# The last quarter-products, the final norm and the stores in a fixed order, with the norm's factors in the last scaling

## The chip, the cores and the metric

The kernel runs on one core of a Trainium2 chip. The metric is the device time of one execution in microseconds (us), the median of several runs. In this text TensorE (PE in the profile) does the matmuls, VectorE (DVE) the elementwise arithmetic, ScalarE (ACT) activations and casts, GpSimd (POOL) some additions, and SyncE (SP) issues the loads and stores.

## What is computed

The reference is one step of a one-layer streaming encoder with 1,024 prompt tokens and 64 sample tokens, 1,088 in all, and a model width of 1,024. Only its end matters here: the SwiGLU block, whose down product is added to the residual stream, and the final RMSNorm with the factors `g_final`.

```python
def rms_norm(x, g=None):
    xf = x.astype(jnp.float32)
    y = xf * lax.rsqrt(jnp.mean(xf * xf, axis=-1, keepdims=True) + EPS)
    if g is not None:
        y = y * g.astype(jnp.float32)
    return y.astype(x.dtype)
...
def swiglu(x, g_ffn, w_gate, w_up, w_down):
    hn = rms_norm(x, g_ffn)
    return (jax.nn.silu(hn @ w_gate) * (hn @ w_up)) @ w_down
...
        hp = hp + swiglu(hp, g_ffn[l], w_gate[l], w_up[l], w_down[l])
...
    y_prompt = rms_norm(hp, g_final)
    y_sample = rms_norm(hs, g_final)
```

## The kernel before

Activations lie transposed: features on the 128 partitions, tokens along the free axis, so the stream is eight tiles `y[0]` to `y[7]` of 128 x 1,088, one for each block of 128 features. Prompt and sample tokens are worked on together. The tokens are cut into two halves of 544 columns (`HALF`), and a half into two quarters of 272 (`HC`). A product in full precision takes three passes: each operand is split into a high and a low part (`split`, L122: a cast on ScalarE, then a subtraction on VectorE, L124), and `mm3` (L147) runs high x high, high x low, low x high.

The instructions are written in Python in some order and a planner then places them: on each engine it takes what is ready in its own simulated timeline, in order of priority, which is the order of writing unless a block raises it (`high_priority`). Where a block stands under `issue_after(ins)`, its instructions on the engine of `ins` may not be placed ahead of `ins`. `in_order` (L855) does so with the last matmul of TensorE that was recorded in `last_mm`. On the chip each engine works through its queue in the order so found, and waits at the head of the queue for what an instruction needs.

The down product (`down`, L1426) runs over the 22 blocks of the hidden width in three groups. Most of it is done by a Strassen scheme of seven half-size products for a pair of feature blocks (`strassen`, L247). In the last group the scheme leaves out the products P2 and P4. With them left out, the second token half (columns 544 to 1,087) is complete after the scheme, and of the first half two partial products are missing; these are computed directly, in the two quarters, from weights that are loaded again (L1490 to L1497). This is the rest: for each quarter eight products of nine matmuls, one for each feature block (L1498 to L1507). A product's result lies in one of four bank pairs of PSUM (the pool `ps`, tag `q`), which is free again when VectorE has added the result to `y` (L1506).

When a feature block of a half or quarter is complete, `complete` (L1442) takes its square on ScalarE (L1446, L1449), adds it to a running sum on VectorE in `self.rstd` (L1450), and multiplies `y` by the factor g of each feature on ScalarE (L1451).

`final_norm` (L1515) then finishes a half or a quarter: matmuls of the sums with ones give each token's sum on the partitions (`token_rstd`, L306), six small steps give the inverse root, with one Newton step (L289 to L294: VectorE, the root on ScalarE, then four on VectorE), matmuls with the identity spread it over the partitions again (L1527), and ScalarE copies it to `self.rstd` (L1528). The whole stands under `high_priority`. `final_scale` (L1530) multiplies the eight tiles by it on VectorE (L1533) and stores each (L1534, issued by SyncE at L120). The order of writing is: rest products of the first quarter; norm and scaling of the second half; norm of the first quarter; rest products of the second quarter; its norm; scaling of the first quarter, then of the second. An activation at L1488 loads the table of the square root early.

## Time and profile before

| what | us |
| --- | --- |
| timed runs | 2256.48, 2258.14, 2258.49 |
| their median | 2258.14 |
| profiled execution | 2251.97 |
| its span from the first to the last instruction or transfer | 2250.1 |

The profiled execution is one run of its own; 1.87 us of it lie outside the span that the profile covers. All times of instructions below are microseconds from the start of this span. A row of a timeline has start, duration, engine, line of the kernel, operation, what it writes and reads with the shapes, how many instructions are merged in it, and in brackets the idle time of the engine ahead of it with what ended that time. A row of a table of groups has, behind the bar, busy time in all and mean nanoseconds of one, and then the idle time ahead. "Clock" is the share of its full clock that TensorE was granted.

### The profile page before, as it was taken

To read this page: it belongs to the slowest core of one execution; us is meant where nothing else is said; L and a number is where in the kernel's file an instruction comes from. 1 tells how busy PE (TensorE), PEld (TensorE's weight loads), DVE (VectorE), ACT (ScalarE), POOL (GpSimd) and SP (SyncE) were. 2 spreads that over 40 slices of the span, in tenths; PEclk is the share of its full clock that TensorE was granted. 3 is DMA by queue.
4 is the path that set the end of the run, shared out by engine and by line. 5 is a ranking of instruction groups with operands and counts; after the bars stand their busy time and mean duration, and the time that the engine had idled before them with its cause. 6 is when DMAs were issued, how large, how long until landed. Compare 5 with 4: busy or idle time off the path is not lost.

```text
span 2250.1 us, 41674 instructions
## 1 busy us (share of the span) xinstructions
PE 2172.4 (97%) x16382; PEld 2108.2 (94%) x16382; DVE 1594.2 (71%) x2656; ACT 896.2 (40%) x1921; POOL 689.0 (31%) x466
## 2 busy tenths in 40 slices
PE   7899999999999989999999999999999999999996
PEld 6899999999999977779999998999999999999996
DVE  8985878677687568875455565776777767777596
ACT  7333333435444355553233343333222223344344
POOL 1441534342253112220000000014555556434471
PEclk9999999999999989999999999999999999999997
DMA  5433344443445475326343111412342332475223
GB/s 199 159 120 109 111 129 130 132 130 113 169 139 187 143 242 164 111 67 222 121 153 113 39 66 59 143 62 91 122 148 79 101 131 85 152 258 192 86 84 108
DMA packets 182598, 290.84 MB, mean 129 GB/s; under 512 B 40290, under 2 KB 110850, under 8 KB 182402
## 3 DMA queue, kind: packets, MB, share of 16 engines
q1 hardware_dynamic: 177794, 279.26, 38.2%
q10 hardware_dynamic: 4608, 8.91, 1.1%
q8 instruction: 129, 2.11, 0.4%
q14 instruction: 67, 0.55, 0.1%
HBM read 196.95 MB, written 91.16 MB: 128 GB/s over the span
## 4 chain that ended last, share of the span: by engine, by line
PE 80%; DVE 10%; DMA 4%; issue 3%; ACT 2%; POOL 1%; SPq 0%; DVEq 0%; ACTq 0%; POOLq 0%
PE pq L205 15%; PE pq L208 15%; PE pq L206 15%; PE pd L149 8%; PE pd L150 8%; PE pd L151 8%; DVE wq L124 2%; PE pout L992 1%; PE pp L976 1%; DMA hl<-d_op 1%; PE pss L934 1%; DVE T L124 1%; DVE B L124 1%; PE pk L691 1%; DVE xg L1280 1%
## 5 line engine op out<-in xcount | busy, mean ns | idle before, releaser
L123 ACT CAST wq<-raw 128x512 fp32r<-128x512 f32 (+1 forms) x505 | 307.9, 614 | 572.1 <-PE pq L208 308.2
L124 DVE TENSOR_TENSOR wq<-raw,wq 128x512 fp32r<-128x512 f32 (+1 forms) x505 | 447.6, 890 | 107.7 <-ACT wq L123 105.7
L205 PE MATMUL pq<-T,wq 128*128 128x272 f32 x1832 | 501.3, 291 | 6.4 <-DVE u L252 3.1
L206 PE MATMUL pq<-T,wq 128*128 128x272 f32 x1832 | 497.7, 288 | 0.0
L205 PE MATMUL pq<-B,wq 128*128 128x272 f32 x1592 | 436.7, 292 | 11.7 <-ACT wq L123 10.5
L206 PE MATMUL pq<-B,wq 128*128 128x272 f32 x1592 | 435.1, 290 | 9.1 <-DVE B L124 8.9
L208 PE MATMUL pq<-T,wq 128*128 128x272 f32 x1832 | 382.6, 289 | 1.0 <-DVE wq L124 0.9
L183 POOL TENSOR_TENSOR raw<-raw 128x512 f32<-128x512 f32 (+1 forms) x59 | 81.6, 1383 | 899.7 <-DVE wq L124 615.2
L205 PEld LDWEIGHTS pq<-T,wq 128*128 128x128 f32 x1832 | 345.2, 188 | 7.2 <-DVE u L252 3.2
L206 PEld LDWEIGHTS pq<-T,wq 128*128 128x128 f32 x1832 | 348.5, 190 | 0.3 <-issue 0.3
L208 PE MATMUL pq<-B,wq 128*128 128x272 f32 x1592 | 333.5, 289 | 0.0
L206 PEld LDWEIGHTS pq<-B,wq 128*128 128x128 f32 x1592 | 304.4, 191 | 11.7 <-DVE B L124 11.3
L205 PEld LDWEIGHTS pq<-B,wq 128*128 128x128 f32 x1592 | 301.3, 190 | 12.4 <-ACT wq L123 10.5
L208 PEld LDWEIGHTS pq<-T,wq 128*128 128x128 f32 x1832 | 285.3, 188 | 2.4 <-DVE wq L124 1.7
L208 PEld LDWEIGHTS pq<-B,wq 128*128 128x128 f32 x1592 | 249.1, 189 | 0.5 <-issue 0.3
L252 DVE TENSOR_TENSOR u<-pq,u 128x544 f32<-128x544 f32 x177 | 127.7, 721 | 128.2 <-PE pq L208 127.5
L186 POOL TENSOR_TENSOR raw<-raw 128x512 f32<-128x512 f32 (+1 forms) x59 | 83.5, 1415 | 141.0 <-DVE wq L124 133.4
L563 DVE TENSOR_TENSOR stage<-pq,u 128x544 f32<-128x544 f32 x112 | 80.4, 718 | 29.1 <-PE pq L208 26.5
L962 POOL TENSOR_TENSOR t<-t,den 128x768 f32<-128x768 f32 (+2 forms) x34 | 47.9, 1409 | 167.5 <-DVE nm L950 58.7
L184 POOL TENSOR_TENSOR raw<-raw 128x512 f32<-128x512 f32 (+1 forms) x59 | 88.3, 1497 | 3.7
L1438 POOL TENSOR_TENSOR y<-u,y 128x544 f32<-128x544 f32 x38 | 63.0, 1664 | 73.6 <-DVE y L1436 51.8
L189 POOL TENSOR_TENSOR raw<-raw 128x512 f32<-128x512 f32 (+1 forms) x59 | 84.1, 1426 | 4.4
(356 smaller groups left out, 4669.8 us busy)
## 6 DMA issues: line engine op xcount, KB each, us to landing
hl<-d_op SPq DMA_DIRECT2D x85, 272.0 KB, 4.1
d_qkv<-stage SPq DMA_DIRECT2D x44, 272.0 KB, 2.1
d_op<-stage SPq DMA_DIRECT2D x44, 272.0 KB, 2.1
d_op<-ht SPq DMA_DIRECT2D x44, 272.0 KB, 3.3
raw<-w_gate SPq DMA_DIRECT2D x22, 512.0 KB, 3.4
raw<-w_up SPq DMA_DIRECT2D x22, 512.0 KB, 3.5
d_gate<-stage ACTq DMA_DIRECT2D x32, 272.0 KB, 2.3
raw<-w_down SPq DMA_DIRECT2D x16, 512.0 KB, 4.3
```

Source lines behind the costliest of these rows:

```text
L123: self.last_cast = self.nc.scalar.copy(hi, src).ins
L124: self.nc.vector.tensor_tensor(out=lo, in0=src, in1=hi.bitcast(F32), op=ALU.subtract)
L149: mm(ps, wh, xh, start=start, stop=False)
L150: mm(ps, wh, xl, start=False, stop=False)
L151: self.last_mm = mm(ps, wl, xh, start=False, stop=stop).ins
L184: tt(out=a21, in0=a21, in1=a22, op=add)
L186: tt(out=a11, in0=a22, in1=a11, op=sub)
L189: tt(out=a12, in0=a12, in1=a11, op=sub)
L205: mm(ps[:, c, :HC], w[:, 0, ks], x[:, 0, cs], start=start, stop=False)
L206: mm(ps[:, c, :HC], w[:, 0, ks], x[:, 1, cs], start=False, stop=False)
L208: self.last_mm = mm(ps[:, c, :HC], w[:, 1, ks], x[:, 0, c * HC:(c + 1) * HC], start=False, stop=stop).ins
L252: add = lambda out, a, b: nc.vector.tensor_tensor(out=out, in0=a, in1=b, op=ALU.add)
```

## The change

The block that finishes the kernel is written anew. `split` now gives back its VectorE instruction, and the last one is recorded in `last_queued`; `queued` writes an instruction of VectorE under `issue_after` of the one recorded before, so that these instructions keep the order of writing. TensorE's part stands under `in_order`. In `finish` the sixteen rest products run one after the other, j = 0 to 15. The half's sums and roots come behind product 5, its spread behind product 7, its eight scalings and stores one by one behind the products 8 to 15; the first quarter's sums and roots behind product 11, its spread behind product 14. The addition of a square comes one product later than the square. Behind the last product stand three scalings of the first quarter, the second quarter's norm, the other five, and the second quarter's eight.

The second quarter's norm (`wide_roots`) takes another way: two matmuls with the 128 x 128 ones, of the running sum and of the last square, give each token's sum on all partitions at once, and the root steps are then done on 128 x 272 instead of 128 x 3, with no spread and no copy.

The multiplication by g on ScalarE (L1451) is gone; `scale` does it together with the norm in one `scalar_tensor_tensor`. The number of stores and their sizes stay.

```diff
     def split(self, src, hi, lo):
         self.last_cast = self.nc.scalar.copy(hi, src).ins
-        self.nc.vector.tensor_tensor(out=lo, in0=src, in1=hi.bitcast(F32), op=ALU.subtract)
+        return self.nc.vector.tensor_tensor(out=lo, in0=src, in1=hi.bitcast(F32), op=ALU.subtract).ins
...
-            nc.scalar.mul(o, o, self.gains[:, 3, m:m + 1])
...
-            self.split(raw[:, :2 * n], q[:, 0, :2 * n], q[:, 1, :2 * n])
+            self.last_queued = self.split(raw[:, :2 * n], q[:, 0, :2 * n], q[:, 1, :2 * n])
             rest += [(m + i, q[:, :, i * n:(i + 1) * n], self.ops[("B21", "T4")[i]]) for i in range(2)]
-        for c0 in (0, HC):
...
-        for c0 in (0, HC):
-            self.final_scale(y, c0, HC)
+        self.finish(y, rest)
+
+    def queued(self, emit):
+        with self.tc.issue_after(self.last_queued):
+            self.last_queued = emit().ins
+
+    def finish(self, y, rest):
         nc = self.nc
+        tt, stt, ts = nc.vector.tensor_tensor, nc.vector.scalar_tensor_tensor, nc.vector.tensor_scalar
+        cols = [slice(0, HC), slice(HC, HALF), slice(HALF, T)]
+        squares, factors = {}, {}
+        bank = lambda: self.bank_pair()[:, 0, :]
+
+        def product(c, m, q, xs):
+            ps = bank()[:, :HC]
+            for k, x in enumerate(xs):
+                ks = slice(k * P, (k + 1) * P)
+                x = x.rearrange("p a (b c) -> p a b c", b=2)[:, :, c]
+                self.mm3(ps, q[:, 0, ks], q[:, 1, ks], x[:, 0], x[:, 1], k == 0, k == len(xs) - 1)
+            return ps
+
+        def grow(c, m, ps):
+            v = y[m][:, cols[c]]
+            self.queued(lambda: tt(out=v, in0=ps, in1=v, op=ALU.add))
+            sq = self.rstd[:, cols[c]]
+            if m:
+                sq = self.hl.tile([P, HALF], F32, tag="hl", name="sq")[:, :HC]
+            nc.scalar.activation(sq, v, AF.Square)
+            squares[c, m] = sq
+
+        def gather(c, m):
+            acc = self.rstd[:, cols[c]]
+            self.queued(lambda: tt(out=acc, in0=acc, in1=squares[c, m], op=ALU.add))
+
+        def sums(c):
+            spans = self.spans(cols[c].stop - cols[c].start)
+            ps = bank()[:, :2 * len(spans)].rearrange("p (t two) -> p t two", two=2)
+            for i, (a, w) in enumerate(spans):
+                a += cols[c].start
+                self.last_mm = nc.tensor.matmul(ps[:, i, :], self.rstd[:, a:a + w], self.ones[:, :2], start=True, stop=True).ins
             r = self.np.tile([P, 5], F32, tag="rf", bufs=2, name="rs_f")[:, :len(spans)]
+            factors[c] = r, spans, ps[:, :, 0]
+
+        def roots(c):
+            r, spans, ps = factors[c]
...
+            self.steps(r, v, t, ps)
+
+        def wide_roots(c, m):
+            ps = bank()[:, :HC]
+            mm = nc.tensor.matmul
+            mm(ps, self.ones, self.rstd[:, cols[c]], start=True, stop=False)
+            self.last_mm = mm(ps, self.ones, squares[c, m], start=False, stop=True).ins
+            v, t = (self.hl.tile([P, HALF], F32, tag="hl", name="wide")[:, :HC] for _ in range(2))
+            self.steps(self.rstd[:, cols[c]], v, t, ps)
+
+        def spread(c):
+            r, spans, _ = factors[c]
+            for part in ((0, 2), (2, 5)) if len(spans) > 4 else ((0, len(spans)),):
+                pb = bank()
+                a0, a1 = spans[part[0]][0], spans[part[1] - 1][0] + P
+                for i in range(*part):
                     at = spans[i][0] - a0
+                    self.last_mm = nc.tensor.matmul(pb[:, at:at + P], r[:, i:i + 1].broadcast_to([P, P]), self.ident,
+                                                    start=True, stop=True).ins
+                c0 = cols[c].start
+                nc.scalar.copy(self.rstd[:, c0 + a0:c0 + a1], pb[:, :a1 - a0])
+
+        def scale(c, k):
+            o = y[k][:, cols[c]]
+            self.queued(lambda: stt(o, o, self.gains[:, 3, k:k + 1], self.rstd[:, cols[c]], ALU.mult, ALU.mult))
+            self.store(self.io["o_y"][k, :, cols[c]], o)
+
+        for j in range(2 * KT):
+            c, m = divmod(j, KT)
+            ps = self.in_order(lambda: product(c, *rest[m]))
+            grow(c, rest[m][0], ps)
+            if (j - 1) % KT and j:
+                gather((j - 1) // KT, rest[(j - 1) % KT][0])
+            if j == 5:
+                self.in_order(lambda: sums(2))
+                roots(2)
+            if j == KT - 1:
+                self.in_order(lambda: spread(2))
+            if j == KT + 3:
+                self.in_order(lambda: sums(0))
+                roots(0)
+            if j == KT + 6:
+                self.in_order(lambda: spread(0))
+            if j >= KT:
+                scale(2, j - KT)
+        for k in range(3):
+            scale(0, k)
+        self.in_order(lambda: wide_roots(1, rest[-1][0]))
+        for k in range(3, KT):
+            scale(0, k)
         for k in range(KT):
+            scale(1, k)
+
+    def steps(self, out, v, t, ps):
+        nc = self.nc
+        stt, q = nc.vector.scalar_tensor_tensor, self.queued
+        q(lambda: nc.vector.tensor_scalar(v, ps, 1.0 / D, EPS, ALU.mult, ALU.add))
+        nc.scalar.activation(out, v, AF.Sqrt)
+        q(lambda: nc.vector.reciprocal(out, out))
+        q(lambda: nc.vector.tensor_tensor(out=t, in0=out, in1=out, op=ALU.mult))
+        q(lambda: stt(t, t, -0.5, v, ALU.mult, ALU.mult))
+        q(lambda: stt(out, t, 1.5, out, ALU.add, ALU.mult))
```

30 lines of the change are left out of this document (2 added, 28 removed).

## The prediction

> **What bounds the kernel now.** I read the page first, then a table by stages of the last 48 us, then those stages instruction by instruction on TensorE, VectorE and the store queue.
>
> ```profile
> span 2250.1 us, 41674 instructions
> PE 2172.4 (97%) x16382; PEld 2108.2 (94%) x16382; DVE 1594.2 (71%) x2656; ACT 896.2 (40%) x1921; POOL 689.0 (31%) x466
> ```
>
> TensorE is busy for 97% of the span, so the kernel as a whole is bound by its matmuls, and the change leaves those as they are. What it can win lies where TensorE isn't busy at the end:
>
> ```profile
> core 0: us, PE busy (x) PEld busy (x) DVE busy (x) ACT busy (x) POOL busy (x), PEclk, DMA share, GB/s
> 2202.40:2209.50 7.10, 4.23 (x29) 3.50 (x28) 5.99 (x8) 3.15 (x4) 2.85 (x2) 0.93 0.31 105
> 2209.50:2215.10 5.60, 5.59 (x24) 5.59 (x25) 4.18 (x9) 5.26 (x13) 1.82 (x2) 0.50 0.00 0
> 2217.90:2226.40 8.50, 4.50 (x33) 4.14 (x33) 6.00 (x19) 2.57 (x8) 0.00 (x0) 0.75 0.23 87
> 2226.40:2229.00 2.60, 2.60 (x13) 2.60 (x13) 2.60 (x6) 0.39 (x1) 0.00 (x0) 0.51 1.03 391
> 2229.00:2236.80 7.80, 7.79 (x63) 7.57 (x61) 6.73 (x18) 5.24 (x14) 0.00 (x0) 1.00 0.61 205
> 2236.80:2243.20 6.40, 2.71 (x12) 2.33 (x12) 2.06 (x8) 1.92 (x5) 0.00 (x0) 0.69 0.01 1
> 2243.20:2250.10 6.90, 0.00 (x0) 0.00 (x0) 2.91 (x8) 0.00 (x0) 0.00 (x0) 0.50 0.47 163
> ```
>
> Each row is a stretch, its length, busy time of each engine and the granted clock. The rest products of the first quarter run to 2217.9. Then 8.5 us pass in which TensorE runs only norm matmuls and waits, 10.4 us with the products of the second quarter, 6.4 us for its norm and 6.9 us for the last scalings and stores. At full clock 63 matmuls take 7.8 us, 0.124 us each, so a product of nine takes 1.12 us.
>
> ```profile
> 2207.35 0.36 PE L149 MATMUL pq<-B,wb 128*128 128x272 f32 x1 [2.02 <-DVE y L1436]
> 2209.51 0.59 PE L149 MATMUL pq<-T,wb 128*128 128x272 f32 x1 [0.69 <-DVE y L1436]
> 2217.84 1.17 PE L306 MATMUL pt<-ones,rstd 128*128 128x2 f32 x10
> 2220.33 0.93 PE L1527 MATMUL pb<-ident,rs_f 128*128 128x128 f32 x6 [1.32 <-DVE rs_f L294]
> 2225.19 1.62 PE L1527 MATMUL pb<-ident,rs_f 128*128 128x128 f32 x6 [2.68 <-DVE rs_f L294]
> 2226.46 0.57 PE L149 MATMUL pq<-B,wb 128*128 128x272 f32 x1
> 2236.51 0.29 PE L151 MATMUL pq<-T,wb 128*128 128x272 f32 x1
> 2238.75 1.06 PE L306 MATMUL pt<-ones,rstd 128*128 128x2 f32 x6 [1.96 <-DVE rstd L1450]
> ```
>
> The second quarter's first product starts at 2226.46, behind spreads that waited for VectorE (2.68 us for a small `rs_f`). VectorE and the store queue in the same stretch and at the end:
>
> ```profile
> 2222.97 0.72 DVE L1533 TENSOR_TENSOR rstd_f<-rstd_f,rstd 128x544 f32<-128x544 f32 x1
> 2224.89 0.15 DVE L294 SCALAR_TENSOR_TENSOR rs_f<-rs_t,rs_f 128x3 f32<-128x3 f32 x1
> 2224.96 3.26 DVE L1533 TENSOR_TENSOR y<-y,rstd 128x544 f32<-128x544 f32 x5
> 2228.49 2.55 DVE L1533 TENSOR_TENSOR y<-y,rstd 128x272 f32<-128x272 f32 x7
> 2243.20 0.44 DVE L1533 TENSOR_TENSOR rstd_f<-rstd_f,rstd 128x272 f32<-128x272 f32 x1 [2.16 <-ACT rstd L1528]
> 2243.56 2.55 DVE L1533 TENSOR_TENSOR y<-y,rstd 128x272 f32<-128x272 f32 x7
> 2243.67 0.33 SPq L120 DMA_DIRECT2D o_y<-rstd_f  x1
> 2244.12 3.55 SPq L120 DMA_DIRECT2D o_y<-y  x7
> ```
>
> That `rs_f` step stood behind scalings of the last half, at 2224.89. But the wait isn't empty time: the eight wide scalings and the first quarter's eight are done in its shadow, so only eight scalings are left for the end. There the queue sets the pace, not VectorE: seven scalings take 2.55 us (0.35 apart), seven stores 3.55 us (0.51 apart). The last issue ends at 2247.67, and 2.43 us later the span ends.
>
> **The change part by part.** *TensorE.* Everything up to 2217.84 is the same work. Into it go the norm matmuls of the half: the sums, ten instructions (1.0 us, as they stand at 2217.84), and the spread, ten instructions at the 0.13 us of the row at 2220.33, 1.3 us. The ninth product therefore starts at 2217.84 + 1.0 + 1.3 = 2220.1 instead of 2226.46. Eight products at full clock, 9.0 us, with six sums (0.6) and six spreads (0.8) between them, end at 2230.5, against 2236.8: 6.3 us earlier.
>
> *VectorE* doesn't keep up. What it does per instruction:
>
> ```profile
> L1450 DVE TENSOR_TENSOR rstd<-rstd,sq 128x272 f32<-128x272 f32 x14 | 6.1, 437 | 1.4 <-ACT sq L1449 1.3
> 1437.97 0.61 DVE L1244 SCALAR_TENSOR_TENSOR xg<-hx,gains,rstd 128x384 f32<-128x384 f32 x1
> 1438.50 0.55 DVE L278 TENSOR_TENSOR rstd_f<-rstd_f,sq 128x384 f32<-128x384 f32 x1
> 2219.05 0.17 DVE L289 TENSOR_SCALAR rs_v<-pt 128x5 f32<-128x5 f32 x1
> 2220.11 0.17 DVE L294 SCALAR_TENSOR_TENSOR rs_f<-rs_t,rs_f 128x5 f32<-128x5 f32 x1
> ```
>
> A narrow `tensor_tensor` takes 0.44 us, and the next one starts after 0.35 to 0.36 (the seven in 2.55 us above). The new scaling multiplies by a column of `gains` too; line 1244 has this form at 384 elements, 0.06 us longer than the `tensor_tensor` behind it. So I take 0.42 for a narrow scaling and, from the 0.64 pitch of the wide ones (five in 3.26 us), 0.70 for a wide one. The five small root steps take 1.2 us from 2219.05 to 2220.11 and its end. From the ninth product on VectorE has 8 adds (2.8), 7 additions of squares (2.5), 8 wide scalings (5.6) and one set of roots (1.3, with its waits): 12.2 us. The first add can start when the ninth product is done, 2220.1 + 1.1 + 0.2 = 2221.4, and the last wide scaling ends at 2233.6, 3.1 us behind TensorE. So VectorE is the bound here, and half of what TensorE wins is gone. The last product's own add, addition and wide scaling need 1.6 us of this, so a delay of TensorE behind the ninth product costs nothing up to 1.5 us and counts in full beyond; one ahead of the ninth product counts in full, since VectorE's row starts with it.
>
> *The last norm* swaps a chain for wider steps. Now: product end 2236.8, add, square, addition, sums at 2238.75, roots, spread, copy, first scaling at 2243.20, 6.4 us. After: the last square and two full-width sums on TensorE run while VectorE does the last wide scaling and three narrow ones, and the roots are taken on all 272 columns.
>
> ```profile
> 1274.31 1.08 PE L1202 MATMUL csss<-ck,qsm 128*64 128x256 f32 x4
> L1449 ACT ACTIVATE sq<-y 128x272 f32<-128x272 f32 x14 | 5.7, 423 | 1.5 <-DVE y L1506 1.3
> L1451 ACT ACTIVATE y<-y,gains 128x272 f32<-128x272 f32 x14 | 6.9, 512 | 0.1
> L291 DVE RECIPROCAL rr<-rr 128x2 f32<-128x2 f32 x16 | 2.6, 162 | 4.3 <-ACT rr L290 4.3
> L291 DVE RECIPROCAL rtok<-rtok 128x8 f32<-128x8 f32 x1 | 0.2, 185 | 0.0
> ```
>
> Two f32 matmuls are four instructions, 1.1 us at this width (1.08 for four of 256); with the square (0.42) and two handovers 1.6 us, hidden behind 0.7 + 3 x 0.42 = 2.0 us of scalings. Then, from 2233.6: three scalings to 2234.9, the affine step to 2235.3, the root on ScalarE (0.42 and two handovers of 0.04) to 2235.8. Nothing else of VectorE may go here, since its order is fixed. A reciprocal of 272 elements is not in the trace. If it runs like a `tensor_tensor`, 0.44 us; by the slope between 2 and 8 elements, 23 ns over six, 0.16 + 270 x 3.8 ns = 1.2, and with 10 ns of doubt on that slope 0.7 to 1.65. I take 1.0, inside the slope's band, and keep 0.44 and 1.65 as ends. Three dependent steps of 0.48 follow: 2238.3. The first scaling behind them ends at 2238.8.
>
> The Trainium skill speaks against the wide reciprocal: "VectorE: DVE Perf Modes", section "Walkthrough: the 8-slice pipeline in each mode", says that it runs as an iterative divide with a repeat count of 8. At its 0.96 GHz that is an estimate of 272 x 8 / 0.96 = 2.3 us, and the sum below would end 1.3 us later. The two rows here agree with something between: 23 ns where the rule gives 50.
>
> *Stores.* Behind that step 13 narrow scalings are left, where there are 8 now. VectorE needs 0.42 for each, the queue 0.51 for each issue, so the queue sets the end: 13 x 0.51 = 6.6, to 2245.5, and 2.4 us until the span ends: 2247.9. The eight wide stores go out earlier, one for every 1.4 us of VectorE, and hide.
>
> *ScalarE* loses 24 multiplications by the gains (0.51 us for a narrow one); it is busy 5.2 of 7.8 us in the last product stage, so that is worth nothing by itself.
>
> *Sum.* TensorE 6.3 us earlier, less 3.1 for VectorE's lag; then 2233.6 to the first free scaling and 13 stores: 2247.9 against 2250.1, 2.2 us less. The profiled execution took 2251.97, 1.87 around its span; the median of the timed runs is 2258.14, 6.2 us above it. I carry the difference over: 2258.14 - 2.2 = 2255.9.
>
> **The rivals.** *The early stalls go too (faster).* TensorE waits 2.02 and 0.69 us at 2207.35 and 2209.51 for additions that stand in VectorE's queue around the splits of the last weights:
>
> ```profile
> 2207.17 1.65 DVE L124 TENSOR_TENSOR wb<-raw,wb 128x768 fp32r<-128x768 f32 x1
> 2208.74 0.71 DVE L1436 TENSOR_TENSOR y<-pq,y 128x544 f32<-128x544 f32 x1
> ```
>
> Behind these waits 25 matmuls run at clock 0.50, 0.227 us each instead of 0.124, 2.5 us. These rows lie ahead of the fixed order. Without ScalarE's multiplications the planner may place splits and additions otherwise. All of it is worth 5.2 us: 2255.9 - 5.2 = 2250.7. Against it: the splits and the additions are written as before, and the weight loads that they wait for too.
>
> *The wide reciprocal is slow.* The rows bound it at 1.65, and if each element takes several times an addition's time the end slips by about 1 us: 2257. The Trainium skill's rule on the divide, named above, points this way.
>
> *The clock stays low (slower).* TensorE has clock 0.75 in the norm stage and 0.51 in the 2.6 us behind it. The new order puts 2.3 us of sums and spreads in one piece ahead of the ninth product. If the second eight products then ran at half clock, 72 x 0.103 = 7.4 us more and 1.4 for their norm matmuls, TensorE would end at 2239.3, and VectorE 1.6 us later instead of at 2233.6: 7.3 us, less the 2.2 won, 2263.2. With 1.5 us of cover and 2.2 won it is slower than before from 3.7 us of such delay on, some 36 matmuls at half clock. Against it: in the trace the half clock stands behind waits, and after 5.6 us of unbroken products it is full again; the spreads follow products at full clock. The Trainium skill ("TensorE: Matmul & The Clock Gate", section "Part 1: The HAM clock gate (the "warmup" mystery)") asks for about 3.4 us of idleness before it halves the clock; here 2.02 and 0.69 us of waits were enough.
>
> *The stall only moves.* The half's spread needs `rs_f` from VectorE, with two products (2.2 us) between its sums and the spread, and two additions, two squares' additions and the 1.2 us of roots in VectorE's queue meanwhile, 2.6 us. If it comes late TensorE waits again, up to the 2.68 us of now, and VectorE's wide scalings with it; the end then slips by 1 to 3 us: 2257 to 2259.
>
> **How the numbers follow.** Forecast 0.46, early stalls 0.18, slow reciprocal 0.18, low clock 0.10, moved stall 0.08. The forecast's own spread is 2 us either way (the reciprocal's ends, 0.6 us; the handovers on a queue of some 45 instructions; the pitch of 13 stores). With the early stalls below and half of the low clock left out, the range is 2250.0 to 2260.5. What a measurement of this kernel can tell from no change is about 0.2%, 4.5 us. Faster by more: nearly all of the early stalls (0.17) and a fifth of the forecast's spread (0.10), 0.27. Slower by more: 0.07 of the low clock and 0.02 of the moved stall, 0.09. Within: 0.64.
>
> **What would show it.** In the changed profile the ninth rest product should start near 2220 with no gap above 0.5 us, and clock 1.00 should hold to the sixteenth. VectorE should have no idle time above 0.5 us from there to the wide root steps, and TensorE should end its products some 3 us ahead of the last wide scaling. The wide reciprocal should show 0.44 to 1.65 us. The last 13 stores should stand 0.5 us apart. I am wrong if TensorE still waits between the two quarters, if additions still stand in front of TensorE and VectorE idles, or if the stretch ahead of 2209.5 has changed.

## The result, and the profile after

The changed kernel took 2250.41 us, the median of six runs (2246.01 to 2252.76), against 2259.95 for the kernel before in runs beside it: a ratio of 0.9952, interval 0.9935 to 0.9969. That is 9.5 us less, where 2.2 were predicted, and beyond both the forecast's own spread and the 0.2% that I called no change. Applied to the 2258.14 us that the prediction started from, the ratio gives 2247.3, below the lower end of its range, 2250.0. The profiled execution took 2246.01.

First the page of the changed kernel, its first lines, and the table by stages of its end (the columns are those shown for before).

```profile
span 2244.2 us, 41644 instructions
PE 2161.9 (96%) x16374; PEld 2097.0 (93%) x16374; DVE 1602.8 (71%) x2655; ACT 883.9 (39%) x1896; POOL 689.8 (31%) x466
```

```profile
core 0: us, PE busy (x) PEld busy (x) DVE busy (x) ACT busy (x) POOL busy (x), PEclk, DMA share, GB/s
2199.70:2205.20 5.50, 2.75 (x18) 2.35 (x19) 4.25 (x6) 2.49 (x4) 0.67 (x1) 1.00 0.50 143
2205.20:2209.00 3.80, 3.65 (x16) 3.35 (x17) 2.86 (x5) 1.20 (x3) 3.80 (x3) 0.56 0.00 0
2209.00:2216.00 7.00, 7.00 (x61) 7.00 (x60) 6.46 (x19) 3.68 (x10) 0.20 (x1) 1.00 0.01 2
2216.00:2226.60 10.60, 10.59 (x87) 10.37 (x85) 8.84 (x24) 3.67 (x10) 0.00 (x0) 1.00 0.31 123
2226.60:2234.70 8.10, 1.47 (x4) 0.68 (x4) 7.50 (x16) 1.29 (x3) 0.00 (x0) 0.68 0.46 167
2234.70:2244.20 9.50, 0.00 (x0) 0.00 (x0) 5.43 (x14) 0.00 (x0) 0.00 (x0) 0.50 0.56 192
```

The 8.5 us in which TensorE ran norm matmuls and waited are gone: from 2209.0 to 2226.6 it is busy throughout at clock 1.00. The work behind its last product, 8.1 us to the first free scaling and 9.5 to the end, is VectorE's and the stores'. Now the timeline of the changed kernel on TensorE, then on VectorE and on the store queue:

```profile
2205.22 0.36 PE L149 MATMUL pq<-B,wb 128*128 128x272 f32 x1 [2.06 <-DVE y L1436]
2211.59 1.17 PE L1540 MATMUL pq<-ones,rstd 128*128 128x2 f32 x10
2214.95 1.27 PE L1566 MATMUL pq<-ident,rs_f 128*128 128x128 f32 x10
2215.99 0.37 PE L149 MATMUL pq<-B,wb 128*128 128x272 f32 x1
2226.30 0.29 PE L151 MATMUL pq<-T,wb 128*128 128x272 f32 x1
2228.77 0.72 PE L1554 MATMUL pq<-rstd,ones 128*128 128x272 f32 x2 [2.18 <-DVE rstd L1532]
```

```profile
2228.63 0.78 DVE L1573 SCALAR_TENSOR_TENSOR y<-y,gains,rstd 128x544 f32<-128x544 f32 x1
2229.32 0.50 DVE L1573 SCALAR_TENSOR_TENSOR rstd_f<-rstd_f,gains,rstd 128x272 f32<-128x272 f32 x1
2230.56 0.44 DVE L1605 TENSOR_SCALAR wide<-pq 128x272 f32<-128x272 f32 x1
2231.49 1.85 DVE L1607 RECIPROCAL rstd<-rstd 128x272 f32<-128x272 f32 x1 [0.49 <-ACT rstd L1606]
2234.69 2.14 DVE L1573 SCALAR_TENSOR_TENSOR y<-y,gains,rstd 128x272 f32<-128x272 f32 x5
2237.17 2.97 DVE L1573 SCALAR_TENSOR_TENSOR y<-y,gains,rstd 128x272 f32<-128x272 f32 x7
2237.59 0.41 SPq L120 DMA_DIRECT2D o_y<-rstd_f  x1
2238.12 3.58 SPq L120 DMA_DIRECT2D o_y<-y  x7
```

The last wide scaling ends at 2229.41, 2.8 us behind TensorE's last product; the wide reciprocal takes 1.85 us; the last stores stand 0.51 us apart (3.58 for seven). The rest begins with a matmul that started at 2202.47 before and starts at 2199.73 now. From there to the end of the span it is 47.7 us before and 44.5 now: 3.2 us are won in this tail, and the other 2.7 us of the two profiles ahead of it.

Up to 2167 us every engine has the same instructions in the same order as before. From there on ScalarE lacks the multiplications and VectorE makes some additions of squares elsewhere, while TensorE's order is the same until the sixth rest product ends. These are the same two matmuls ahead of any difference, before and after:

```profile
2165.34 0.52 PE L208 MATMUL pq<-T,wq 128*128 128x272 f32 x2 [0.19 <-DVE wq L124]
2161.83 0.52 PE L208 MATMUL pq<-T,wq 128*128 128x272 f32 x2 [0.20 <-DVE wq L124]
```

In this pair of profiles 3.5 us were won by the same instructions in the same order, and had to come from something else. The two programs differ in one more thing. The part of `roots` that the diff above leaves out reads

```python
            v = self.np.tile([P, 5], F32, tag="vf", bufs=2, name="rf_v")[:, :len(spans)]
            t = self.np.tile([P, 5], F32, tag="tf", bufs=2, name="rf_t")[:, :len(spans)]
```

Two new tags with two buffers each are four tiles of 20 bytes, given 32 bytes each, in the pool `norm`. That pool is opened near the front of the kernel, so all tiles that are laid out behind it on that side (the loaded weights `raw`, their split parts `wq`, sums, stages) lie 128 bytes further along each partition; the large operands `B` and `T` are laid out from the other side and stay.

### The profile page after: what moved, and what is told of

The parts are those of the page before. It is cut to its first block, busy times and chain, and to the rows that moved or that the text cites. A ratio compares the mean times of both kernels' runs of the same rounds, so it can differ in the third digit from the quotient of the medians.

```text
span 2244.2 us, 41644 instructions
## 1 busy us (share of the span) xinstructions
PE 2161.9 (96%) x16374; PEld 2097.0 (93%) x16374; DVE 1602.8 (71%) x2655; ACT 883.9 (39%) x1896; POOL 689.8 (31%) x466
## 4 chain that ended last, share of the span: by engine, by line
PE 80%; DVE 10%; DMA 4%; issue 2%; ACT 2%; POOL 1%; SPq 0%; DVEq 0%; ACTq 0%; POOLq 0%
PE pq L208 15%; PE pq L205 15%; PE pq L206 15%; PE pd L149 8%; PE pd L151 8%; PE pd L150 8%; DVE wq L124 2%; PE pout L992 1%; DMA hl<-d_op 1%; PE pp L976 1%; PE pss L934 1%; DVE T L124 1%; DVE B L124 1%; DMA qs<-d_qkv 1%; PE pk L691 1%
## 5 line engine op out<-in xcount | busy, mean ns | idle before, releaser
L124 DVE TENSOR_TENSOR wq<-raw,wq 128x512 fp32r<-128x512 f32 (+1 forms) x505 | 456.6, 908 | 126.4 <-ACT wq L123 124.2
L205 PE MATMUL pq<-T,wq 128*128 128x272 f32 x1832 | 492.5, 289 | 5.6 <-DVE u L252 3.7
L206 PE MATMUL pq<-T,wq 128*128 128x272 f32 x1832 | 492.8, 289 | 0.0
L206 PE MATMUL pq<-B,wq 128*128 128x272 f32 x1592 | 430.1, 290 | 9.7 <-DVE B L124 9.5
L205 PE MATMUL pq<-B,wq 128*128 128x272 f32 x1592 | 428.0, 289 | 11.8 <-ACT wq L123 10.6
L208 PE MATMUL pq<-T,wq 128*128 128x272 f32 x1832 | 384.1, 290 | 3.6 <-DVE wq L124 3.6
L205 PEld LDWEIGHTS pq<-T,wq 128*128 128x128 f32 x1832 | 346.0, 189 | 6.3 <-DVE u L252 3.7
L206 PEld LDWEIGHTS pq<-T,wq 128*128 128x128 f32 x1832 | 346.0, 189 | 0.3 <-issue 0.3
L208 PE MATMUL pq<-B,wq 128*128 128x272 f32 x1592 | 334.2, 290 | 0.0
L206 PEld LDWEIGHTS pq<-B,wq 128*128 128x128 f32 x1592 | 301.2, 189 | 12.2 <-DVE B L124 11.8
L205 PEld LDWEIGHTS pq<-B,wq 128*128 128x128 f32 x1592 | 300.8, 189 | 12.5 <-ACT wq L123 10.6
L208 PEld LDWEIGHTS pq<-T,wq 128*128 128x128 f32 x1832 | 291.0, 190 | 5.1 <-DVE wq L124 4.4
L208 PEld LDWEIGHTS pq<-B,wq 128*128 128x128 f32 x1592 | 253.5, 190 | 0.5 <-issue 0.3
```

The source lines that it names most:

```text
L124: return self.nc.vector.tensor_tensor(out=lo, in0=src, in1=hi.bitcast(F32), op=ALU.subtract).ins
L205: mm(ps[:, c, :HC], w[:, 0, ks], x[:, 0, cs], start=start, stop=False)
L206: mm(ps[:, c, :HC], w[:, 0, ks], x[:, 1, cs], start=False, stop=False)
L208: self.last_mm = mm(ps[:, c, :HC], w[:, 1, ks], x[:, 0, c * HC:(c + 1) * HC], start=False, stop=stop).ins
```

## The experiments

Every ratio is against the kernel before on the same chip, with its 95% interval. "Start" is the start of the first rest product, "tail" from there to the end of the span, and "behind six" the part of the tail behind the sixth rest product, where TensorE's orders part; each is read from the one profiled execution of that kernel. "Stretch" is the time from the 240th to the 360th DMA issue, from about 494 to 738 us, where TensorE runs products without a pause.

| kernel | tiles moved by | ratio | start | tail | behind six | stretch |
| --- | --- | --- | --- | --- | --- | --- |
| before (profile ahead) | 0 | | 2202.5 | 47.7 | 34.6 | 244.08 |
| again_before | 0 | 1.0002 (0.9991 to 1.0012) | 2203.7 | 48.1 | 36.2 | 244.08 |
| gains_only | 0 | 0.9995 (0.9986 to 1.0003) | 2209.6 | 49.7 | 36.3 | 244.08 |
| after_noshift | 0 | 0.9991 (0.9982 to 1.0000) | 2209.3 | 44.4 | 32.6 | 244.07 |
| late_128 | 0, others 128 | 1.0009 (1.0000 to 1.0019) | 2206.6 | 48.8 | 35.9 | 244.11 |
| shift_32 | 32 | 1.0004 (0.9994 to 1.0014) | 2209.0 | 45.1 | 36.2 | 244.09 |
| shift_64 | 64 | 1.0013 (1.0003 to 1.0023) | 2206.5 | 48.1 | 36.3 | 243.88 |
| shift_160 | 160 | 1.0003 (0.9993 to 1.0012) | 2207.5 | 47.6 | 37.4 | 244.26 |
| shift_96 | 96 | 0.9952 (0.9939 to 0.9966) | 2196.9 | 46.6 | 37.6 | 241.62 |
| shift_only | 128 | 0.9969 (0.9957 to 0.9981) | 2201.1 | 47.7 | 37.3 | 242.34 |
| after (profile above) | 128 | 0.9952 (0.9935 to 0.9969) | 2199.7 | 44.5 | 32.6 | 242.34 |
| again_after | 128 | 0.9966 (0.9953 to 0.9979) | 2201.2 | 46.1 | 32.6 | 242.34 |
| order_only | 128 | 0.9953 (0.9940 to 0.9966) | 2201.2 | 44.5 | 31.8 | 242.34 |
| narrow | 128 | 0.9955 (0.9941 to 0.9968) | 2199.0 | 45.2 | 31.7 | 242.34 |
| pe_order | 128 | 0.9972 (0.9961 to 0.9983) | 2199.6 | 48.1 | 34.5 | 242.34 |
| dve_order | 128 | 0.9962 (0.9948 to 0.9975) | 2204.7 | 46.2 | 32.6 | 242.42 |
| best | 128 | 0.9938 (0.9926 to 0.9951) | 2200.0 | 39.6 | 30.2 | 242.34 |
| after_96 | 96 | 0.9933 (0.9919 to 0.9946) | 2197.7 | 44.7 | 32.6 | 241.61 |
| best_96 | 96 | 0.9907 (0.9894 to 0.9921) | 2191.8 | 40.2 | 29.8 | 241.98 |

**Is it the tail alone?** Two runs repeat the kernels, two take the change apart.

> The kernel before, unchanged, timed against itself. It shows what a ratio of this kernel is worth. Theory A (the tail alone is shorter, by some 3 us, and the rest of the measured 0.48% is scatter of the runs ahead of the tail): ratio 0.998 to 1.002, but single runs spread by 4 us or more, and the profile's start of the rest products (2202.5 before, 2199.7 after the change) falls anywhere between 2198 and 2206. Theory B (the changed build is also faster ahead of the tail): runs spread little and the rest products start near 2202.5 again.

> The changed kernel once more. Theory A: ratio about 0.9985 (3.2 us of 2258), between 0.997 and 1.000, and the stretch from the first rest product to the end of the span 44 to 46 us again. Theory B: ratio near 0.995 again, and the first rest product starts 3 us or more earlier than in the unchanged kernel on the same chip.

gains_only is the kernel before with the factors in its last scaling:

```diff
-            nc.scalar.mul(o, o, self.gains[:, 3, m:m + 1])
...
-            tt(out=o, in0=o, in1=self.rstd[:, cols], op=ALU.mult)
+            stt(o, o, self.gains[:, 3, m:m + 1], self.rstd[:, cols], ALU.mult, ALU.mult)
```

order_only is the changed kernel with the factors left with ScalarE:

```diff
+            nc.scalar.mul(o, o, self.gains[:, 3, m:m + 1])
...
+            nc.scalar.mul(v, v, self.gains[:, 3, m:m + 1])
...
-            self.queued(lambda: stt(o, o, self.gains[:, 3, k:k + 1], self.rstd[:, cols[c]], ALU.mult, ALU.mult))
+            self.queued(lambda: tt(out=o, in0=o, in1=self.rstd[:, cols[c]], op=ALU.mult))
```

> The kernel before, with only the factors moved from ScalarE into the last scaling. My sum puts nothing on it: ratio 0.999 to 1.001, tail 47 to 49 us, TensorE's wait between the quarters as before (some 8 us). Rival: ScalarE's multiplications held up casts, and their removal is what pays: ratio below 0.998 and a tail below 46 us.

> The changed kernel with the factors left on ScalarE (squares and then the multiplication there, a tensor_tensor as the last scaling). My sum: nearly all of the gain is the order, so ratio within 0.001 of the changed kernel's, tail 43.5 to 46 us. Scalings 0.06 us shorter each on VectorE (0.5 us over the eight wide ones). Rival as above: the gain goes and the tail is back at 47 us.

Moving the factors alone does nothing that the ratio can tell from no change, though the tail of its one profile, 49.7 us, is above the 47 to 49 expected; order_only has the whole gain. So the gain isn't ScalarE's 24 multiplications, as predicted. And the ratio of again_after says that it isn't the tail alone, as theory A had it; again_after and order_only reach the rest 1.3 to 2.5 us earlier than the two profiles of before, if not by the 3 that theory B asked for. The groups of scalings on VectorE, order_only first, then the changed kernel, show what the factors cost there:

```profile
L1575 DVE TENSOR_TENSOR y<-y,rstd 128x272 f32<-128x272 f32 x14 | 5.2, 435 | 0.0
L1575 DVE TENSOR_TENSOR y<-y,rstd 128x544 f32<-128x544 f32 x7 | 5.0, 718 | 0.0
```

```profile
L1573 DVE SCALAR_TENSOR_TENSOR y<-y,gains,rstd 128x272 f32<-128x272 f32 x14 | 6.0, 494 | 0.0
L1573 DVE SCALAR_TENSOR_TENSOR y<-y,gains,rstd 128x544 f32<-128x544 f32 x7 | 5.5, 780 | 0.0
```

That is 0.06 us for each of 24 scalings, 1.4 us of VectorE's time, for work that ScalarE had room for. Behind the sixth product order_only takes 31.8 us against 32.6, 0.8 less; the ratios are too wide to show it.

**Is it where the tiles lie?** shift_only gives before's final norm the changed kernel's four small tiles and nothing else (t is edited like v):

```diff
+        self.last_norm = False
...
-        v = self.np.tile([P, 16], F32, tag="v", bufs=2, name="rs_v")[:np_, :n]
...
+        w, f = (5, "f") if self.last_norm else (16, "")
+        v = self.np.tile([P, w], F32, tag="v" + f, bufs=2, name="rs_v")[:np_, :n]
...
+        self.last_norm = True
```

after_noshift lets the changed kernel's roots use the old tags (t like v again):

```diff
-            v = self.np.tile([P, 5], F32, tag="vf", bufs=2, name="rf_v")[:, :len(spans)]
+            v = self.np.tile([P, 16], F32, tag="v", bufs=2, name="rf_v")[:, :len(spans)]
```

> The kernel before with the same instructions in the same order; the final norm's roots alone take their two working tiles (v and t) from four new tiles of 5 columns, so that every tile behind the pool "norm" lies 128 bytes further along each partition, as in the changed kernel. Theory C (the part of the gain that lies ahead of the rest products comes from these addresses): ratio to before 0.9980 to 0.9987 (3 to 4.5 us faster), the first rest product starts near 2200 to 2201 us, the tail from there keeps its 48 us. Theory D (addresses mean nothing, and what lies ahead of the tail is scatter or another property of the changed program): ratio 0.9990 to 1.0010, first rest product 2202.5 to 2204.

> The changed kernel, its final roots working in the old tiles of 16 columns, so that all tiles lie where they lay before; order and instructions are those of the changed kernel. Theory C: only the tail's gain is left, ratio to before 0.9982 to 0.9990 (2.2 to 4 us faster), first rest product 2202.5 to 2204, tail 44.5 to 46. Theory D: as the changed kernel, ratio 0.9953 to 0.9970, first rest product 2199.5 to 2201.5.

Theory C holds, and by more than it asked for: the move alone is worth 0.0031 of 2256 us, 7.0 us (interval 4.3 to 9.7, where 3 to 4.5 were expected), and without it the changed kernel wins 0.0009, 2.0 us (0 to 4.1). The starts of single profiles are poor evidence: after_noshift's, 2209.3, is far beyond the 2202.5 to 2204 expected. The stretch tells more. These are the two DMA issues that bound it and a group of TensorE's products between them, for before, then for the changed kernel:

```profile
494.23 0.36 SPq L117 DMA_DIRECT2D ks<-d_qkv  x1
738.30 0.33 SPq L117 DMA_DIRECT2D raw<-w_gb  x1
L205 PE MATMUL pq<-T,wq 128*128 128x272 f32 x303 | 82.9, 291 | 0.0
```

```profile
493.88 0.36 SPq L117 DMA_DIRECT2D ks<-d_qkv  x1
736.22 0.33 SPq L117 DMA_DIRECT2D raw<-w_gb  x1
L205 PE MATMUL pq<-T,wq 128*128 128x272 f32 x303 | 81.2, 288 | 0.0
```

738.30 less 494.23 is 244.07, 736.22 less 493.88 is 242.34. Five profiles with the weights in their old place have 244.07 to 244.11, eight with all moved by 128 bytes have 242.34 to 242.42, whatever they do at the end. TensorE has no idle time there, and the same number of matmuls, before and after:

```profile
494.23:738.30 244.07, 244.07 (x1950) 242.15 (x1949) 179.92 (x273) 113.08 (x201) 86.56 (x57) 1.00 0.45 148
493.88:736.22 242.34, 242.34 (x1950) 240.44 (x1950) 179.78 (x273) 112.97 (x201) 86.12 (x57) 1.00 0.46 149
```

So it is TensorE's own pace that changes, at a clock of 1.00 in both. The pace is the time from one matmul's start to the next one's; the durations in the rows overlap and don't give it. L205 is the first of a product's three passes (high x high), L206 the second, L208 the third (low x high). From start to start they take 127.8, 125.1 and 126.0 ns on average before, and 123.8, 125.5 and 126.7 after: the first pass is 4.0 ns faster, the others 0.4 and 0.7 slower.

**Which tiles, and how far?** One small tile widened moves everything behind it. In shift_64 it is v of the norm's steps; shift_32 widens another tile of that pool, `row`, which has one buffer, from 16 to 24 columns; shift_96 does both, shift_160 both with v at 32.

```diff
-        v = self.np.tile([P, 16], F32, tag="v", bufs=2, name="rs_v")[:np_, :n]
+        v = self.np.tile([P, 24], F32, tag="v", bufs=2, name="rs_v")[:np_, :n]
```

late_128 puts 128 empty bytes behind the weights' pool, so that only what lies behind the weights moves:

```diff
             self.wp = ctx.enter_context(self.tc.tile_pool(name="weights", bufs=2, reuse_waits="tile"))
+            pad = ctx.enter_context(self.tc.tile_pool(name="pad", bufs=1, reuse_waits="tile"))
+            pad.tile([P, 32], F32, name="pad")
```

> The kernel before, one small working tile of the norms widened from 16 to 24 columns (two buffers), so that every tile behind it lies 64 bytes further; no instruction changes. Theory C1 (the addresses of before are an unlucky set, and nearly any other is faster): ratio 0.9965 to 0.9980. Theory C2 (what counts is the place in blocks of 128 bytes or more, so 64 is half way or undoes itself): 0.9980 to 1.0020. Theory D (not addresses, but the four new tiles themselves): 0.9990 to 1.0010 with each engine's pace as before; the 1625 products between 494 and 738 us would then take 288.7 ns each as before, and not 287.8 as in all builds that moved by 128 bytes.

> The kernel before, another small tile of the norms (one buffer) widened by 8 columns, so that every tile behind it lies 32 bytes further; no instruction changes. Theory C1 (any other addresses than those of before are faster): ratio 0.9965 to 0.9980. Theory C2 (tiles that no longer begin on 64 bytes cost more): 1.0000 to 1.0040, with longer weight loads or products. Theory D: 0.9990 to 1.0010.

> The kernel before with an empty tile of 128 bytes behind the pool of the weights: the weights and their raw halves lie where before has them, and only the tiles behind them (sums, stage, squares, ring heads on that side) lie 128 bytes further. No instruction changes. Theory W (what counts is where the weights lie that TensorE loads and that VectorE and ScalarE write): the stretch from the 240th to the 360th DMA issue takes 244.1 us as in all builds with the addresses of before, ratio 0.9990 to 1.0010. Theory L (the other tiles): 242.3 us there as in all builds moved by 128 bytes, ratio 0.9960 to 0.9980.

> The kernel before, two small working tiles of the norms widened so that every tile behind them lies 160 bytes further. No instruction changes. If places in blocks of 128 bytes decide, 160 goes with 128: ratio 0.9960 to 0.9985 and 242.3 to 242.6 us in the stretch from the 240th to the 360th DMA issue. If the place within 128 bytes decides, it goes with 32: 1.0000 to 1.0010 and 244.1 us.

> As the one before, by 96 bytes. If the effect grows in steps between 64 (243.88 us in the stretch, ratio 1.0013) and 128 (242.34 us, 0.9969), 96 lies between them: 243 us and 0.9990. If each place has its own cost without an order, any value from 0.9965 to 1.0015.

The same rows of late_128, then of shift_96:

```profile
497.34 0.36 SPq L117 DMA_DIRECT2D ks<-d_qkv  x1
741.45 0.33 SPq L117 DMA_DIRECT2D raw<-w_gb  x1
L205 PE MATMUL pq<-T,wq 128*128 128x272 f32 x303 | 82.9, 291 | 0.0
```

```profile
496.48 0.36 SPq L117 DMA_DIRECT2D ks<-d_qkv  x1
738.10 0.33 SPq L117 DMA_DIRECT2D raw<-w_gb  x1
L205 PE MATMUL pq<-T,wq 128*128 128x272 f32 x303 | 81.3, 287 | 0.0
```

late_128 takes 244.11 us and has before's 291 ns, so the tiles behind the weights don't matter by themselves, and the place of the weights does. The step isn't smooth: 32, 64 and 160 bytes are worth nothing or cost a little, 96 more than 128 (241.62 us against 242.34 in the stretch). shift_160 goes with shift_32, as it would if the place within 128 bytes decided; but then a move by 128 would be worth nothing, and it is worth 7.0 us. Which pass is slow depends on the place: 125.2, 123.4 and 125.9 ns in shift_96, 127.1, 126.5 and 125.2 in shift_160. shift_96, before with two padded tiles and no other change, is as fast as the whole change (0.9952). Only the last expectation allowed for places without an order, and the ratio that came, 0.9952, lies below its lower bound of 0.9965.

**What carries the tail's own gain?** pe_order is the changed kernel with TensorE's order fixed and VectorE's left to the planner:

```diff
-        with self.tc.issue_after(self.last_queued):
-            self.last_queued = emit().ins
+        self.last_queued = emit().ins
```

dve_order is the reverse; `in_order` is taken from the products and likewise from sums, spreads and the wide roots:

```diff
-            ps = self.in_order(lambda: product(c, *rest[m]))
+            ps = product(c, *rest[m])
```

> The changed kernel with TensorE's order fixed as it is, and VectorE's left to the planner, which puts the wide scalings of the second quarter ahead of some of the adds of its y. Theory 1 (the gain of the tail comes from TensorE's order, in which no product waits for a norm): tail 44 to 46.5 us, ratio to before within 0.0010 of the changed kernel's. Theory 2 (VectorE's fixed order carries it): scalings that wait for the spread roots hold up adds and sums behind them, tail 46.5 to 48.5 us, ratio 0.0010 to 0.0020 above the changed kernel's.

> The changed kernel with VectorE's order fixed as it is and TensorE's left to the planner, the other half of the kernel with only TensorE's order fixed, whose tail was 48.05 us and whose ratio was 0.9972, no better than the shifted addresses alone (0.9969). Theory 1 (VectorE's order carries the tail's gain): tail 44.5 to 46.5 us, ratio 0.9950 to 0.9966. Theory 2 (both are needed, neither alone gives any of it): tail 47 to 49 us, ratio 0.9965 to 0.9980.

dve_order came out of the planner with the changed kernel's order on every engine, so it is a third measurement of it (0.9952, 0.9966, 0.9962), and with VectorE's order fixed nothing had to be asked of TensorE. pe_order has the same order on TensorE too, but its tail is 48.1 us, no gain at all, and its ratio is that of the moved tiles alone. Behind the sixth product it takes 34.5 us, where the changed order takes 32.6 and before's profile 34.6. VectorE's and TensorE's timelines of pe_order say why:

```profile
2219.14 4.96 DVE L1572 SCALAR_TENSOR_TENSOR y<-y,gains,rstd 128x544 f32<-128x544 f32 x7
2224.01 0.44 DVE L1522 TENSOR_TENSOR rstd_f<-pq,rstd_f 128x272 f32<-128x272 f32 x1
2224.51 0.83 PE L1539 MATMUL pq<-ones,rstd 128*128 128x2 f32 x6 [2.16 <-DVE rstd_f L1522]
```

The planner puts all the wide scalings in one piece ahead of the second quarter's additions. TensorE, four result banks later, waits 2.16 us for the first of these additions. The order that pays is the one that keeps the scalings between the additions. Whether TensorE's order is worth anything by itself is open: the other profiles of the old order take 35.9 to 37.6 us behind the sixth product, more than pe_order's 34.5.

**The wide roots.** narrow is the changed kernel with the first quarter's narrow norm for the second too:

```diff
-        self.in_order(lambda: wide_roots(1, rest[-1][0]))
+        gather(1, rest[-1][0])
+        self.in_order(lambda: sums(1))
         for k in range(3, KT):
             scale(0, k)
+        roots(1)
+        self.in_order(lambda: spread(1))
```

> The changed kernel, but the norm of the second quarter by narrow sums, narrow roots and a product that spreads them, as that of the first quarter has it, instead of the wide sums and wide roots. The wide roots took 4.13 us on VectorE behind the last wide scaling in the changed kernel's profile, of which 1.85 us is the reciprocal. Theory 1 (VectorE's wide steps set the end there): five narrow steps, which TensorE and ScalarE answer in between, take about 0.3 us each and the spread product about 0.7 us with its wait, so about 2.5 to 3 us in place of 4.1, and the time falls by 0.5 to 2 us against the changed kernel (ratio to before about 0.9950 to 0.9965 where the changed kernel has 0.9966). Theory 2 (the hops between engines cost as much as the wide steps): within 0.5 us of the changed kernel, or up to 2 us slower.

Its time can't be told from the changed kernel's; behind the sixth product its one profile takes 31.7 us against 32.6. In its timeline the short roots end 2.2 us before VectorE can go on:

```profile
2234.81 0.16 DVE L1613 SCALAR_TENSOR_TENSOR rs_f<-rf_t,rs_f 128x3 f32<-128x3 f32 x1
2237.13 0.50 DVE L1573 SCALAR_TENSOR_TENSOR rstd_f<-rstd_f,gains,rstd 128x272 f32<-128x272 f32 x1 [2.16 <-ACT rstd L1569]
```

Most of what the wide reciprocal costs, the spread and its copy cost again when nothing covers them. So best asks for the sums early and leaves five scalings to run beside the spread; it keeps the factors on ScalarE and lets ScalarE issue every second one of the last 16 stores. Against order_only:

```diff
-            self.store(self.io["o_y"][k, :, cols[c]], o)
+            issue = nc.scalar.dma_start if c < 2 and k % 2 else nc.sync.dma_start
+            issue(self.io["o_y"][k, :, cols[c]], o)
...
+        gather(1, rest[-1][0])
+        self.in_order(lambda: sums(1))
         for k in range(3):
             scale(0, k)
-        self.in_order(lambda: wide_roots(1, rest[-1][0]))
+        roots(1)
+        self.in_order(lambda: spread(1))
```

after_96 and best_96 are the changed kernel and best with the tiles moved by 96 bytes: rf_t takes the old tag t, which leaves 64, and `row` is 24 wide, which adds 32.

> order_only (the fixed order, the factors left with ScalarE) with the second quarter's norm by narrow sums, roots and a spread product, the sums asked for ahead of the first quarter's scalings and the spread behind three of them, and every second one of the last 16 stores issued by ScalarE instead of SP. From order_only's trace: its VectorE works 10.0 us from the end of the last wide scaling to the last narrow one; here a gather (0.35), sixteen scalings at a pitch of 0.35 (5.6) and five narrow root steps with their hops (1.2) are 7.2 us, if the spread (2.3 us behind the roots in the kernel with the narrow norm) lies behind the five scalings left (1.8). So 2.2 to 2.8 us less than order_only, tail 41.5 to 42.5 us, ratio to before 0.9938 to 0.9946. Rival (the queue of stores or the hops set the end): tail 43.5 to 45 us, ratio 0.9950 to 0.9960.

> The changed kernel with every tile behind the pool "norm" 96 bytes further than before has it, instead of 128. If the order's gain and the addresses' gain add: 0.9952 of shift_96 less 0.0009 (2.0 us, the order at the addresses of before) is 0.9943, with the scatter of the runs 0.9930 to 0.9955. If the order gives nothing of its own: 0.9945 to 0.9965. The stretch from the 240th to the 360th DMA issue takes 241.6 us as in shift_96, against 242.3 at 128 bytes.

> best (0.9938 at 128 bytes) at 96 bytes. If the gains add: 0.9938 less 0.0017 (0.9969 of 128 bytes to 0.9952 of 96) is 0.9921, with scatter 0.9908 to 0.9935, about 2238 us. If the weights' place matters less under the other order: 0.9935 to 0.9945.

The timeline of best_96, VectorE, then the two issuing queues:

```profile
2222.83 1.84 DVE L1575 TENSOR_TENSOR y<-y,rstd 128x272 f32<-128x272 f32 x5
2225.02 0.44 DVE L1575 TENSOR_TENSOR rstd_f<-rstd_f,rstd 128x272 f32<-128x272 f32 x1 [0.35 <-ACT rstd L1571]
2225.38 2.55 DVE L1575 TENSOR_TENSOR y<-y,rstd 128x272 f32<-128x272 f32 x7
2226.20 1.74 SPq L1577 DMA_DIRECT2D o_y<-y  x3
2224.70 3.59 ACTq L1577 DMA_DIRECT2D o_y<-y  x5
```

best has the ratio that was expected. Its tail, 39.6 us, is shorter than the 41.5 to 42.5 worked out, as is best_96's, 40.2. But behind the sixth product the two take 30.2 and 29.8 us, 1.6 and 2.0 less than order_only's 31.8, where 2.2 to 2.8 were expected; the rest of the shorter tails lies ahead of what best changes. The wait of 2.16 us is down to 0.35, the scalings stand 0.35 us apart instead of 0.41, and the last issue ends at 2228.3, 0.4 us behind the last scaling, instead of 1.6 (2241.70 against 2240.14 in the changed kernel). The new norm and the second issuing engine weren't timed apart. With the tiles moved by 96 bytes the time is 2234.49 us (2233.87 to 2236.05), 0.9907, faster than both kernels: the gains add, to a little more than the 0.9921 expected.

## Why the prediction was wrong

The step that failed is the first of the part on TensorE: "Everything up to 2217.84 is the same work." TensorE's work is the same, and I carried its time over as the same, into the sum ("I carry the difference over") and into the rivals, none of which reached further ahead than the early stalls. The runs put 7.0 us there (4.3 to 9.7): shift_only, with no instruction changed, has 0.9969, and in the one stretch that could be compared TensorE's pace is what changes. The text named this as what would make it wrong ("if the stretch ahead of 2209.5 has changed") without a cause for it or a price. The whole diff has the new tags, and what a new tile moves could have been asked. What it would be worth could not: at the five distances tried it was between +0.0013 and -0.0048, and only runs gave that.

What was left, the order's own worth, came out near the prediction. At the same places of the tiles the changed order is worth 0.0009 (0.9991 against 1), 0.0009 (the mean of 0.9952, 0.9966 and 0.9962 against 0.9969) and 0.0019 (0.9933 against 0.9952): 2.0, 2.0 and 4.3 us, against 2.2. Each of the three has an interval of 2 us or more either way, so none shows it alone. The tails say the same: five profiles of the changed order have 44.4 to 46.2, mean 45.2; eight of the old have 45.1 to 48.8, mean 47.4: 2.3 us.

Some of that agreement is luck. Behind the sixth product the five take 32.6 us, all of them, and the eight 34.6 to 37.6, mean 36.5. The sum was made from the shortest of the eight: before's profile has its norms' half clock from 2222.1 to 2229.0, 6.9 us, where again_before has it for 10.2 (2220.5 to 2230.7) and shift_only too (2218.8 to 2229.0). These are the start of the seventh product and the two stretches, the clock third from the right, for before, before and again_before:

```profile
2215.57 0.29 PE L149 MATMUL pq<-B,wb 128*128 128x272 f32 x1
2222.10:2229.00 6.90, 4.22 (x20) 3.95 (x19) 6.53 (x15) 0.95 (x3) 0.00 (x0) 0.51 0.66 252
2220.50:2230.70 10.20, 7.52 (x34) 7.25 (x35) 6.96 (x17) 1.36 (x4) 0.00 (x0) 0.50 0.48 183
```

Against that profile the changed order wins 2.0 us there, against the mean 3.9. Ahead of it, from the first rest product to the end of the sixth, the five take 12.6 us on average and the eight 11.0, mostly by how long the half clock behind the early stalls lasts: in the first pair of profiles 1.2 of the 3.2 us won come from this.

Point by point, in the changed profile:

- *Ninth product.* Predicted 17.6 us behind the first rest product (2220.1 less 2202.47), measured 16.3 (2215.99 less 2199.73); the sums and spreads ahead of it take 1.04 us each until the next product starts, where 1.0 and 1.3 were put. The shorter half-clock stretch is the rest. No wait stands between the quarters: the rival of the moved stall fell.
- *Clock.* 1.00 from 2209.0 to 2226.6: the rival of the low clock fell. Early stalls: 2.06 us are still there ahead of 2205.22, so that rival fell as well; that its 2250.7 is near what came out is an accident.
- *VectorE is the bound.* Ninth to last product 10.6 us (10.4 predicted), VectorE 2.8 us behind (3.1). pe_order bears it out: with VectorE's order left to the planner, the part behind the sixth product is 1.9 us longer.
- *The wide reciprocal.* 1.85 us, above the 0.44 to 1.65 that I bounded it with and 0.85 over the 1.0 in the sum: the term of the tail that was mis-sized; the last wide scaling's end to the first free scaling is 5.3 us, where the sum has 4.7. It is 6.8 ns for each of 272 elements, where an addition takes 1.6 (437 ns for 272); the slope between 2 and 8 elements (3.8 ns) didn't carry. The rule of the Trainium skill ("VectorE: DVE Perf Modes", section "Walkthrough: the 8-slice pipeline in each mode") gave an estimate of 2.3; the measurement lies between and nearer to the rule. This rival was right that an element costs several times an addition's time, and its 1 us was hidden in 7 of another kind.
- *Scalings and stores.* 0.41 and 0.69 us apart (0.42 and 0.70 predicted), the stores 0.51, the span's end 2.5 us behind the last issue (2.4).
- *ScalarE's multiplications* are worth nothing that the ratios show: gains_only 0.9995, order_only as good as the changed kernel.

Open is the mechanism of the place: that it is the weights' place and that TensorE's pace changes with it is shown; why some distances help and others don't, and whether it is the loads into `raw`, the splits or TensorE's own reads, is not. The stretch explains 1.7 us of the 7. By the 960th DMA issue, near 2140 us, the means of the five and the eight profiles are 5.6 us apart, but single profiles of one place differ by 5 to 6 there, too much to place the rest. Open too is whether moving the factors lengthens the half clock behind the early stalls: from the first rest product to the end of the sixth, the eight profiles without ScalarE's multiplications take 12.9 us on average and the eleven with them 11.0, but gains_only's ratio shows no loss. The Trainium skill ("SBUF — State Buffer", section "SBUF: two separate sides") lets engines hinder each other only at the ports that VectorE and GpSimd share; no run here tells whether these take part.

## What to carry to other kernels

A change that allocates anything, even 128 bytes of small tiles, also moves what is laid out behind it, and in this kernel, whose TensorE is busy for 96% of the span, that alone was worth from +0.13% to -0.48%. Measure an edit beside a build with the same instructions and the edit's addresses (or the edit with the old ones) before its gain is put down to its idea, and when a kernel is done, try a few paddings: here 96 bytes gave as much as the whole rewrite. Where one engine trails another through a stage, fix the order on the one that trails.

## What was not expected of the hardware

- At a granted clock of 1.00 TensorE's pace still depends on where the weights lie: the first pass of a product took 127.8, 123.8 or 125.2 ns a matmul with the tiles moved by 0, 128 or 96 bytes. The stretch that the products fill repeats to a tenth of a microsecond between kernels of one place (244.07 to 244.11, 242.34 to 242.42), except at 96 bytes (241.61, 241.62 and 241.98).
- Stalls of the same length cost differently from run to run. Behind waits of 2.0 and 0.8 us ahead of the sixth product TensorE's clock stayed at 1.00 in shift_only, shift_160 and best_96, and was 0.50 for 3.4 us in again_before (from 2210.3) and for 6.8 us in again_after (from 2207.8).
- The fastest place had no better clock: shift_96's runs had a mean granted clock of 0.985, those of before beside them 0.986, and took 10 us less.
- A reciprocal costs VectorE 1.85 us where a multiplication of the same 128x272 takes 0.44.
